# Dilated mixers with masks added by TensorE and the softmax read from PSUM; p's upper parts copied bank by bank

## The chip, the core and the metric

The kernel runs on one core of a Trainium2 chip. The core has five instruction queues that run beside each other and wait for each other by semaphores: TensorE (PE in the profile; PEld is its weight load), VectorE (DVE), ScalarE (ACT), GpSimd (POOL) and SyncE (SP, which issues DMAs). Each queue runs its instructions in order. The metric is device microseconds of one execution.

## The reference, cut to what matters

Two models run one after the other on 1024 positions of width 1024, all in fp32. The first has a differential attention layer (layer 0) and a latent attention layer (layer 1, MLA: 8 heads, softmax over the whole row of 1024 keys). The second has a block with three mixers (A: spatial gating, B: stick-breaking attention, 6 heads, C: dilated attention, 6 heads in 3 groups) and a feed-forward part (FFN). The two softmaxes that the change touches:

```python
# MLA, a head and a block of 128 queries
p = softmax((qn @ kn.T + qp @ kpe.T) * scale); o = p @ v

# mixer C, dilation d = 1, 4, 16 by group: each query sees itself and up to 128 keys, d apart, before it
z = where(valid, (q * k_gathered).sum(-1) * 0.125, -inf)
z_max = z.max(-1); p = exp(z - z_max); denom = p.sum(-1)
o = (p @ v_gathered) / denom;  lse = z_max + log(denom)
alpha = softmax(lse over the 3 groups);  y_c = o * alpha
```

## The kernel before, in words

Every fp32 operand of a product is split into an upper part, rounded to the type that TensorE reads fast (F32R), and a rest, the lower part; a product is two or three matmuls of such parts. The split of a tile in PSUM is an ACT copy (the upper part) and a DVE subtraction (`lo`, the lower part). In the profile a split of p is "ACT CAST pt<-m" and "DVE TENSOR_TENSOR pt<-m,pt".

The order on each engine is not written by hand: the kernel is written as generators that are merged, and a scheduler then sets the order of the instructions by a simulated timeline and priorities. So a change of one function can move instructions anywhere near. PSUM is held by four pools: tiles s (scores, two buffers of two banks), m (four buffers of one bank), t and u (two each). A tile's buffer is free for the next tile when its last reader is done. All instructions go through one wrapper at line 111, so the profile's rows all carry L111 and are told apart by tiles: s scores, e the row of exponentials, pt the split p, v the values, cf small columns of numbers, cr the identity matrix, kk/qq mixer keys and queries, h the split keys and queries of MLA, wr/wh/wl weights as loaded and their upper and lower part, tf/tb/z/t/ab work tiles.

In time order: layer 0 runs to about 1040 us, layer 1 with MLA to 1500 us, its output product and the mixers' start to 1630 us, the dilated mixers C to about 1830 us, mixer B to 2100 us, then the FFN.

MLA (`mla_attention`): for each head and block of 128 queries, 10 matmuls write a tile s of 128x1024 scores; DVE takes the row maximum from PSUM, ACT the exponential from PSUM with its sum; POOL multiplies by the reciprocal of the sum; `pt_fill` then transposes p with TensorE, four blocks of 128 columns into one bank m, twice for a row. For each bank it issues copy, lo, copy, lo: one pair for the first two blocks and one for the others. Mixer B uses the same `pt_fill`; layer 0 doesn't.

Mixer C (`mixer_c_attention`): three groups with dilations d = 1, 4 and 16, two heads e in each, two halves of four query blocks in each head; so 12 halves, of which the 8 with d < 16 are wide (256 key columns a block) and 4 narrow (128). Each half makes its scores with two matmuls a block in a tile s (`score`, start to stop), copies them to SBUF with ACT (one copy for the own blocks, one for the blocks before), masks the copies with GpSimd (`affine_select`, `memset`), and then runs maximum, subtraction, exponential, sum on DVE, DVE, ACT, DVE. After both halves of a head come the logarithm (ACT), a scalar_tensor_tensor and a reciprocal (DVE), all into one small tile `ld` with a single buffer, and DMAs on SyncE's queue that scatter its two halves into a DRAM tensor lse. So a second head's logarithm and reciprocal wait until the first head's DMAs have read `ld`. When the third group is done, `alphas_c` loads lse back and takes the softmax over the groups on DVE and ACT.

The change also touches `mask_tile`, which makes mixer B's triangular mask, and `load`, which gives a tile whose first uses in a part of the program are tied to a column `sign` by a small GpSimd copy, so that they can't be made earlier than that column.

## Time and profile before

| | us |
|---|---|
| runs of the kernel | 2916.08, 2925.15, 2933.8 (median 2925.15) |
| profiled execution, its own time | 2909.92 |
| its span (first to last instruction) | 2907.9 |
| TensorE busy / VectorE / ScalarE / GpSimd in the span | 2629.5 / 2099.3 / 1421.6 / 1292.2 |
| mean granted TensorE clock, share of full speed | 0.956 |

TensorE is busy for 90% of the span, VectorE for 72%, ScalarE for 49%, GpSimd for 44%. Times in the rows are microseconds from the span's start. An idle stretch of an engine is put down to the engine whose work ended it. The granted clock is 1.0 at 2.4 GHz and 0.5 at 1.2 GHz; a stretch's value is the mean.

### The profile page before, as it was taken

What the parts mean: (1) busy time and instruction counts of PE and PEld (TensorE: products, weight loads), DVE (VectorE), ACT (ScalarE), POOL (GpSimd) and SP (SyncE); (2) the same over time, 40 slices, a digit from 0 to 9 for tenths busy, and PEclk for the clock granted to TensorE, in tenths of its full rate; (3) what the DMA queues carried; (4) which work ended last, traced back from release to release, by engine and by line L of the source; (5) the groups of instructions that cost most, each with busy time, mean ns of one, the idle gap of its engine ahead of it and who ended that gap; (6) DMA issues with size and microseconds to landing.
All of it is one profiled execution on the core that took longest, in us unless ns stands there. A gap on an engine that the chain in (4) does not pass through costs nothing. (4 is left out here: it accounts for less than half of the span.)

```text
span 2907.9 us, 34523 instructions
## 1 busy us (share of the span) xinstructions
PE 2629.5 (90%) x12023; PEld 2128.7 (73%) x12023; DVE 2099.3 (72%) x2696; ACT 1421.6 (49%) x2609; POOL 1292.2 (44%) x779
## 2 busy tenths in 40 slices
PE   7899999998899979999997798887978999997897
PEld 4678787887777867877775687776766777776676
DVE  7577877778642596667768563778768888899865
ACT  5455555556444534544554453667544344443432
POOL 2423323342344532212243332444447878778761
PEclk8999999999999999999998999999989999998998
DMA  7233333234541473223342356332621222234564
GB/s 292 66 97 101 109 109 105 66 95 141 174 131 42 127 254 106 71 89 118 117 132 80 80 82 112 91 87 85 197 89 51 88 79 73 87 124 146 187 237 147
DMA packets 308402, 338.91 MB, mean 117 GB/s; under 512 B 37428, under 2 KB 232068, under 8 KB 308228
## 3 DMA queue, kind: packets, MB, share of 16 engines
q1 hardware_dynamic: 308228, 336.69, 39.3%
q8 instruction: 96, 1.57, 0.2%
q14 instruction: 78, 0.64, 0.1%
HBM read 231.17 MB, written 60.89 MB: 100 GB/s over the span
## 5 line engine op out<-in xcount | busy, mean ns | idle before, releaser
L111 PE MATMUL m<-h,wh 128*128 128x512 f32 x3480 | 985.0, 402 | 48.1 <-DVE h L111 14.4
L111 PEld LDWEIGHTS m<-h,wh 128*128 128x128 f32 x3480 | 669.4, 194 | 204.2 <-DVE h L111 18.2
L111 POOL TENSOR_TENSOR wl<-wr,wh 128x1024 fp32r<-128x1024 f32 (+1 forms) x146 | 333.5, 2291 | 429.6 <-ACT wh L111 393.4
L111 PE MATMUL u<-h,wh 128*128 128x512 f32 x1264 | 408.3, 404 | 1.4 <-ACT h L111 0.8
L111 POOL TENSOR_SCALAR e<-e,cf 128x1024 f32<-128x1024 f32 x128 | 152.6, 1193 | 564.8 <-DVE cf L111 403.5
L111 PE MATMUL m<-h,wl 128*128 128x512 f32 x840 | 336.8, 402 | 7.8 <-POOL wl L111 7.8
L111 ACT ACTIVATE e<-s,cf 128x1024 f32<-128x1024 f32 x192 | 216.0, 1126 | 240.4 <-DVE cf L111 221.9
L111 ACT CAST wh<-wr 128x1024 fp32r<-128x1024 f32 (+3 forms) x252 | 202.6, 810 | 170.1 <-PE m L111 67.7
L111 DVE TENSOR_REDUCE cf<-s 128x1 f32<-128x1024 f32 x192 | 228.3, 1217 | 69.6 <-PE s L111 69.2
L111 PEld LDWEIGHTS u<-h,wh 128*128 128x128 f32 x1264 | 233.1, 191 | 47.5 <-ACT h L111 1.2
L111 PE MATMUL u<-h,wl 128*128 128x512 f32 x632 | 252.5, 400 | 12.7 <-POOL wl L111 12.7
L111 PE MATMUL s<-kk,qq 128*128 128x512 f32 (+3 forms) x752 | 187.3, 386 | 35.8 <-DVE e L111 18.7
L111 ACT CAST pt<-m 128x256 fp32r<-128x256 f32 (+2 forms) x396 | 140.1, 376 | 155.1 <-PE m L111 88.4
L111 PE MATMUL s<-h,wh 128*128 128x512 f32 x720 | 182.8, 399 | 35.5 <-DVE h L111 18.2
L111 PEld LDWEIGHTS m<-h,wl 128*128 128x128 f32 x840 | 164.1, 195 | 44.5 <-POOL wl L111 9.0
L111 DVE SCALAR_TENSOR_TENSOR e<-z,cf,e 128x1023 f32<-128x1023 f32 (+1 forms) x88 | 175.8, 2008 | 24.8 <-ACT e L111 24.6
L111 PE MATMUL s<-h,h 128*128 128x512 f32 x640 | 171.5, 414 | 20.8 <-DVE h L111 14.3
L111 PEld LDWEIGHTS s<-h,wh 128*128 128x128 f32 x720 | 136.5, 192 | 71.3 <-DVE h L111 19.7
L111 DVE TENSOR_TENSOR pt<-m,pt 128x256 fp32r<-128x256 f32 (+2 forms) x396 | 155.0, 416 | 41.6 <-ACT pt L111 34.6
L111 PEld LDWEIGHTS s<-kk,qq 128*128 128x128 f32 x752 | 135.9, 196 | 65.8 <-DVE e L111 20.4
L111 PE MATMUL m<-pt,v 128*128 128x512 f32 (+3 forms) x668 | 151.9, 371 | 17.1 <-ACT pt L111 8.6
L111 PEld LDWEIGHTS s<-h,h 128*128 128x128 f32 x640 | 122.3, 196 | 52.5 <-DVE h L111 17.8
(285 smaller groups left out, 4848.0 us busy)
## 6 DMA issues: line engine op xcount, KB each, us to landing
wr<-in_w_in_dram SPq DMA_DIRECT2D x61, 512.0 KB
wr<-in_w_out_dram SPq DMA_DIRECT2D x48, 512.0 KB
tb<-in_w_ada_dram SPq DMA_DIRECT2D x48, 512.0 KB
wr<-in_w_up_dram SPq DMA_DIRECT2D x47, 512.0 KB
qq<-ab SPq DMA_DIRECT2D x144, 128.0 KB
wr<-in_ada_w_dram SPq DMA_DIRECT2D x32, 512.0 KB
tf<-act SPq DMA_DIRECT2D x30, 512.0 KB
wr<-in_w_down_dram SPq DMA_DIRECT2D x30, 512.0 KB
```

What stands on the lines that cost most here:

```text
L111: ins = f(*args, **kw)
```

## The change

Three functions change, and one is new.

`pt_fill`: the upper parts of a bank are copied one behind the other, then the lower parts are taken: copy, copy, lo, lo in place of copy, lo, copy, lo. The number of instructions stays.

`mixer_c_attention`: in each block of a half an additional matmul of the identity with a mask tile comes first (start) and writes 0 or a large negative number, and the two score matmuls add to it. DVE takes the maximum straight from PSUM and a small scaling by -0.125 of it; four exponentials (ACT, one for each block, since the bias is a column for each block) read PSUM, write the tile e and give the sums. The ACT copies, GpSimd's masks and memsets on the scores, the DVE subtraction and the DVE sum go.

`masks_c` (new): five mask blocks made on GpSimd in a tile z at the mixers' start and copied by ACT into a tile tb that stays for all three groups.

`mask_tile`: its tile comes from `load`, so the mask for mixer B is made at the mixers' start and not at the program's.

```diff
@@ -280,7 +280,7 @@
     def mask_tile(self, name, op, pattern, mult):
 
         nc = self.nc
-        m = self.t("t2", [128, 128])
+        m = self.load("t2", [128, 128])
         nc.gpsimd.memset(m, 0.0)
         nc.gpsimd.affine_select(m, m, pattern, op, -BIG, base=0, channel_multiplier=mult)
         out = self.c([128, 128], name, F32R)
@@ -820,11 +820,11 @@
             for i in range(n):
                 kt = 4 * g + i
                 nc.tensor.transpose(ps[:, i], p[:, kt * 128:(kt + 1) * 128], self.ident)
-            for i in range(0, n, 2):
-                m = min(2, n - i)
-                hi, lo = (pts[4 * g + i + x][:, 0:m, qs] for x in range(2))
-                nc.scalar.copy(hi, ps[:, i:i + m])
-                self.lo(lo, ps[:, i:i + m], hi)
+            parts = [(pts[4 * g + i], pts[4 * g + i + 1], i, min(2, n - i)) for i in range(0, n, 2)]
+            for hi, _, i, m in parts:
+                nc.scalar.copy(hi[:, 0:m, qs], ps[:, i:i + m])
+            for hi, lo, i, m in parts:
+                self.lo(lo[:, 0:m, qs], ps[:, i:i + m], hi[:, 0:m, qs])
 
     def pv(self, v, pts):
 
@@ -1826,7 +1826,21 @@
             qf = [lambda hl, j, s=s: qt[s][hl][:, j * 128:j * 128 + 128] for s in range(2)]
         box += [kk, qf]
 
-    def mixer_c_attention(self, g, d, kk, q, vbox, lse, od):
+    def masks_c(self):
+
+        nc = self.nc
+        m = self.load("z", [128, 5, 128])
+        nc.gpsimd.memset(m, 0.0)
+        nc.gpsimd.affine_select(m[:, 0], m[:, 0], [[1, 128]], ALU.is_ge, -BIG, base=0, channel_multiplier=-1)
+        for i in (1, 3, 4):
+            nc.gpsimd.affine_select(m[:, i], m[:, i], [[-1, 128]], ALU.is_ge, -BIG, base=0, channel_multiplier=1)
+        nc.gpsimd.memset(m[:, 2], -BIG)
+        nc.gpsimd.memset(m[64:128, 4, 0:64], -BIG)
+        out = self.t("tb", [128, 5, 128], F32R)
+        nc.scalar.copy(out, m)
+        return out
+
+    def mixer_c_attention(self, g, d, kk, q, vbox, lse, od, masks):
         nc = self.nc
         y = self.t("z", [128, S])
         wide = d < 16
@@ -1838,33 +1852,24 @@
                 np_ = 2 if wide else 1
                 ps = self.pS((128, 4, 256))
                 z = self.t("e", [128, 4, np_, 128])
-                for i, j in enumerate(js):
-                    k0 = j * 128 - (128 if prev(j) else 0)
-                    o = ps[:, i, 256 - (j * 128 + 128 - k0):256]
-                    self.score(o, q[e], j, kk[e], slice(k0, j * 128 + 128))
-                own = z[:, :, np_ - 1]
-                nc.scalar.copy(own, ps[:, :, 128:256])
-                nc.gpsimd.affine_select(own, own, [[0, 4], [-1, 128]], ALU.is_ge, -BIG, base=0, channel_multiplier=1)
-                if not wide:
-                    nc.gpsimd.memset(own[64:128, :, 0:64], -BIG)
-                else:
-                    sel = [i for i, j in enumerate(js) if prev(j)]
-                    off = [i for i in range(4) if i not in sel]
-                    sl = slice(sel[0], sel[-1] + 1, sel[1] - sel[0])
-                    pz = z[:, sl, 0]
-                    nc.scalar.copy(pz, ps[:, sl, 0:128])
-                    nc.gpsimd.affine_select(
-                        pz, pz, [[0, len(sel)], [1, 128]], ALU.is_ge, -BIG, base=0, channel_multiplier=-1)
-                    for i in off:
-                        nc.gpsimd.memset(z[:, i, 0], -BIG)
-                z3 = z.rearrange("p j a k -> p j (a k)")
                 wd = np_ * 128
                 zm = stat[:, half * 4:half * 4 + 4]
                 den = stat[:, 8 + half * 4:12 + half * 4]
-                nc.vector.reduce_max(zm, z3, axis=AX)
-                nc.vector.tensor_sub(z3, z3, zm.rearrange("p (j o) -> p j o", o=1).to_broadcast([128, 4, wd]))
-                nc.scalar.activation(z3, z3, AF.Exp, scale=0.125)
-                nc.vector.reduce_sum(den, z3, axis=AX)
+                nm = self.small(4, "ss")
+                for i, j in enumerate(js):
+                    m = (0 if prev(j) else 2) if wide else 4
+                    nc.tensor.matmul(ps[:, i, 256 - wd:256], self.ident_r, masks[:, m:m + np_], start=True, stop=False)
+                    k0 = j * 128 - (128 if prev(j) else 0)
+                    ks = slice(k0, j * 128 + 128)
+                    o = ps[:, i, 256 - (j * 128 + 128 - k0):256]
+                    nc.tensor.matmul(o, q[e](0, j), kk[e][:, ks], start=False, stop=False)
+                    nc.tensor.matmul(o, q[e](1, j), kk[e][:, ks], start=False, stop=True)
+                zs = ps[:, :, 256 - wd:256]
+                nc.vector.reduce_max(zm, zs, axis=AX)
+                nc.vector.tensor_scalar_mul(nm, zm, -0.125)
+                for i in range(4):
+                    nc.scalar.activation(z[:, i].rearrange("p a k -> p (a k)"), zs[:, i], AF.Exp, bias=nm[:, i:i + 1],
+                                         scale=0.125, accum_out=den[:, i:i + 1])
                 parts = [[i for i, j in enumerate(js) if prev(j)] if a_ == 0 and wide else list(range(4))
                          for a_ in range(np_)]
                 o = self.pm()
@@ -1944,6 +1949,7 @@
 
         vcol = lambda i: 2432 + i * 128 if i < 3 else 1280 + (i - 3) * 128
         self.off_b = self.mask_tile("off_b", ALU.is_gt, [[-1, 128]], 1)
+        masks = self.masks_c()
         ma = self.mixer_a(w, hts, od)
         def qkv(i, box, vbox):
             yield from qk(i, box)
@@ -1957,7 +1963,7 @@
             cur, cv, box, vbox = box, vbox, [], []
             nxt = qkv(i + 1, box, vbox)
             if i < 3:
-                att = self.mixer_c_attention(i, dil[i], *cur, cv, lse, od)
+                att = self.mixer_c_attention(i, dil[i], *cur, cv, lse, od, masks)
                 merge(ahead(self.tc, att, HP_C), alternate(ma, nxt) if i == 0 else nxt, LEAD_C)
             else:
                 att = self.mixer_b_attention(i - 3, *cur, cv, od)
```

The instructions of all engines stand in the same order up to about 1055 us (layer 1's first head) and again from about 2190 us on (the FFN); between them the scheduler has set another order. TensorE has 48 more matmuls (7066 rows of the order for 6999), VectorE 2610 rows for 2625, ScalarE 2342 for 2356, GpSimd 754 for 776.

Three places show it, all on VectorE's queue. The first stands before layer 1's last head, before and then after; pt are the lower parts of p, m_11977 and m_11986 the two banks of one row of p, h the lower part of that head's queries and keys, cf<-s a row maximum:

```order
L111 TENSOR_TENSOR pt_11892<-m_11977,pt_11891 128x2x128
L111 TENSOR_TENSOR pt_11896<-m_11986,pt_11895 128x2x128
L111 TENSOR_TENSOR h_2006_12055<-tf_12053,h_2006_12055 128x512
L111 TENSOR_TENSOR h_2007_12058<-tf_12053,h_2007_12058 128x512
L111 RECIPROCAL cf<-cf 128x1
L111 TENSOR_REDUCE cf<-s_12334 128x1
L111 TENSOR_SCALAR cf<-cf 128x1
L111 TENSOR_TENSOR h_2013_12098<-tf_12096,h_2013_12098 128x512
L111 TENSOR_REDUCE cf<-s_12407 128x1
L111 TENSOR_TENSOR h_2014_12101<-tf_12096,h_2014_12101 128x512
L111 TENSOR_TENSOR pt_11894<-m_11977,pt_11893 128x2x128
L111 TENSOR_TENSOR pt_11898<-m_11986,pt_11897 128x2x128
```

```order
L111 TENSOR_TENSOR pt_11892<-m_11977,pt_11891 128x2x128
L111 TENSOR_TENSOR pt_11894<-m_11977,pt_11893 128x2x128
L111 TENSOR_TENSOR pt_11896<-m_11986,pt_11895 128x2x128
L111 TENSOR_TENSOR pt_11898<-m_11986,pt_11897 128x2x128
L111 TENSOR_TENSOR h_2006_12055<-tf_12053,h_2006_12055 128x512
L111 TENSOR_TENSOR h_2007_12058<-tf_12053,h_2007_12058 128x512
L111 TENSOR_REDUCE cf<-s_12261 128x1
L111 RECIPROCAL cf<-cf 128x1
L111 TENSOR_SCALAR cf<-cf 128x1
L111 TENSOR_TENSOR h_2013_12098<-tf_12096,h_2013_12098 128x512
L111 TENSOR_REDUCE cf<-s_12334 128x1
L111 TENSOR_TENSOR h_2014_12101<-tf_12096,h_2014_12101 128x512
```

The second subtractions of both banks stood ten rows behind the first ones; now the four follow each other, ahead of the work on h.

The second place is the end of the first head's softmax in the second dilated group (d=4). RECIPROCAL and SCALAR_TENSOR_TENSOR on cf of 128x8 write `ld`, tf are the rotated queries and keys of the next group, z the head's output; tile numbers differ between the two kernels by a small offset (z_13969 is z_13989). Before, and then after:

```order
L111 TENSOR_TENSOR z_13969<-m_14271,t_2359_14304 64x512
L111 RECIPROCAL cf<-cf 128x8
L111 SCALAR_TENSOR_TENSOR cf<-cf 128x8
L111 SCALAR_TENSOR_TENSOR tf_14384<-m_14358,tb_12737 128x512
L111 TENSOR_TENSOR tf_14383<-m_14358,tb_12736 128x512
L111 TENSOR_REDUCE cf<-e_14729 128x4
L111 SCALAR_TENSOR_TENSOR cf<-cf 128x8
L111 TENSOR_TENSOR tf_14444<-m_14394,tb_12736 128x512
L111 TENSOR_TENSOR tf_14445<-m_14394,tb_12737 128x512
L111 RECIPROCAL cf<-cf 128x8
```

```order
L111 SCALAR_TENSOR_TENSOR cf<-cf 128x8
L111 TENSOR_REDUCE cf<-s_14726 128x4
L111 TENSOR_SCALAR cf<-cf 128x4
L111 RECIPROCAL cf<-cf 128x8
L111 SCALAR_TENSOR_TENSOR cf<-cf 128x8
L111 TENSOR_TENSOR z_13989<-m_14281,t_2361_14314 64x512
L111 TENSOR_TENSOR tf_14393<-m_14343,tb_12736 128x512
L111 TENSOR_TENSOR tf_14394<-m_14343,tb_12737 128x512
L111 SCALAR_TENSOR_TENSOR tf_14394<-m_14368,tb_12737 128x512
L111 TENSOR_TENSOR tf_14393<-m_14368,tb_12736 128x512
```

Before, the second head's RECIPROCAL (the last row) stood behind four rows on tf; now it stands (fourth row) three rows behind the row that ends the first head's `ld`, and ahead of the z row and all four tf rows.

The third place is the end of the third group (d=16), second head. tb and e of 128x128 to 128x384 belong to mixer B, ab to mixer B's projections. Before, and then after:

```order
L111 TENSOR_REDUCE cf<-e_15098 128x4
L111 TENSOR_REDUCE cf<-e_15137 128x4
L111 SCALAR_TENSOR_TENSOR tb_15206<-cf,tb_15206 128x128
L111 SCALAR_TENSOR_TENSOR tb_15264<-cf,tb_15264 128x256
L111 TENSOR_TENSOR e_15098<-e_15098,cf 128x512
L111 TENSOR_TENSOR e_15137<-e_15137,cf 128x512
L111 SCALAR_TENSOR_TENSOR tb_15281<-cf,tb_15281 128x384
L111 TENSOR_REDUCE cf<-e_15098 128x4
L111 TENSOR_REDUCE cf<-e_15137 128x4
L111 TENSOR_TENSOR z_14926<-m_15037,t_2467_15054 64x8x64
L111 RECIPROCAL cf<-cf 128x8
L111 SCALAR_TENSOR_TENSOR cf<-cf 128x8
```

```order
L111 TENSOR_REDUCE cf<-s_15133 128x4
L111 TENSOR_REDUCE cf<-s_15093 128x4
L111 TENSOR_SCALAR cf<-cf 128x4 x2
L111 RECIPROCAL cf<-cf 128x8
L111 TENSOR_TENSOR z_14493<-m_14746,t_2428_14773 64x2x256
L111 SCALAR_TENSOR_TENSOR cf<-cf 128x8
L111 SCALAR_TENSOR_TENSOR ab_14823<-m_14798,ab_14823 128x512
L111 SCALAR_TENSOR_TENSOR ab_14851<-m_14826,ab_14851 128x512
L111 SCALAR_TENSOR_TENSOR ab_14889<-m_14864,ab_14889 128x512
L111 TENSOR_TENSOR pt_14947<-m_14942,pt_14947 128x512
L111 TENSOR_SCALAR e_15201<-s_15197 128x128
L111 SCALAR_TENSOR_TENSOR ab_14917<-m_14892,ab_14917 128x512
```

Before, the second head's softmax stood between rows of mixer B, and `alphas_c`'s first reduce 12 rows behind the last row shown; now it stands ahead of all of mixer B, and that reduce 27 rows behind its SCALAR_TENSOR_TENSOR on cf (the sixth row).

## Rows read from the trace of the kernel before

**Rows 1.** Busy time of the engines in stretches of the span: from:to, length, then busy us of each engine with its instructions, TensorE's granted clock as a share of full speed, DMA share and GB/s.

```profile
1100.00:1200.00 100.00, 96.02 (x489) 79.50 (x488) 67.05 (x140) 48.81 (x117) 21.64 (x21) 0.98 0.32 94
...
1630.00:1830.00 200.00, 185.56 (x936) 156.04 (x937) 106.00 (x139) 85.28 (x138) 62.20 (x55) 0.95 0.56 104
1830.00:2120.00 290.00, 246.45 (x1200) 203.65 (x1199) 231.98 (x317) 189.07 (x369) 128.05 (x70) 0.94 0.40 115
```

**Rows 2.** Waits from 1100 to 1500 us (layer 1's attention), all engines: engine and the tile it wrote, the engine waited for and the tile that it wrote, us in total, times, longest.

```profile
ACT pt L111 <- DVE pt L111: 44.2, 49, 2.4
...
DVE pt L111 <- ACT pt L111: 24.0, 30, 3.0
...
PE s L111 <- DVE h L111: 8.5, 3, 3.5
...
PE m L111 <- DVE v L111: 3.4, 1, 3.4
```

**Rows 3.** The same view as rows 1, for three short stretches just behind long waits of TensorE (two in layer 1's attention, one at the start of mixer B).

```profile
1140.40:1143.80 3.40, 3.40 (x12) 2.82 (x11) 3.40 (x6) 0.97 (x3) 0.00 (x0) 0.50 0.80 272
...
1433.90:1440.70 6.80, 5.90 (x18) 4.67 (x19) 5.98 (x17) 3.35 (x9) 2.23 (x2) 0.50 1.00 339
1853.80:1860.60 6.80, 5.39 (x14) 4.43 (x15) 6.55 (x13) 4.82 (x12) 1.44 (x2) 0.50 0.31 86
```

**Rows 4.** Timeline of VectorE from 1424 to 1434 us, before layer 1's last head: start, us, engine, operation, out<-in, shape, count [idle before <- releaser].

```profile
1424.83 0.75 DVE L111 TENSOR_TENSOR pt<-m,pt 128x256 fp32r<-128x256 f32 x2
...
1428.17 2.86 DVE L111 TENSOR_TENSOR h<-tf,h 128x512 fp32r<-128x512 f32 x1
...
1432.68 0.74 DVE L111 TENSOR_TENSOR pt<-m,pt 128x256 fp32r<-128x256 f32 x2
...
1434.08 0.67 DVE L111 TENSOR_TENSOR v<-m,v 128x512 fp32r<-128x512 f32 x1
```

**Rows 5.** The same view of TensorE at 1434.8 us.

```profile
1434.80 1.12 PE L111 MATMUL m<-cr,e 128*128 128x128 f32 x4 [3.37 <-DVE v L111]
```

**Rows 6.** Instructions grouped by form from 1630 to 1835 us (the dilated mixers): line, engine, operation, out<-in, shape, count | busy us, mean ns | idle before.

```profile
L111 DVE TENSOR_REDUCE cf<-e 128x4 f32<-128x1024 f32 x16 | 19.3, 1216 | 5.8 <-POOL e L111 3.1 <-ACT e L111 2.6
...
L111 DVE TENSOR_TENSOR e<-e,cf 128x1024 f32<-128x1024 f32 x8 | 9.7, 1220 | 0.0
L111 POOL TENSOR_SCALAR_AFFINE_SELECT e<-e 128x512 f32<-128x512 f32 x14 | 9.1, 666 | 18.6 <-ACT e L111 18.6
...
L111 ACT ACTIVATE e<-e 128x1024 f32<-128x1024 f32 x8 | 8.4, 1060 | 8.2 <-DVE e L111 8.2
...
L111 ACT COPY e<-s 128x512 f32<-128x512 f32 x14 | 7.9, 604 | 5.7 <-PE s L111 3.9 <-remote 1.8
...
L111 DVE TENSOR_REDUCE cf<-e 128x4 f32<-128x512 f32 x8 | 5.1, 675 | 0.2 <-ACT e L111 0.2
...
L111 DVE TENSOR_TENSOR e<-e,cf 128x512 f32<-128x512 f32 x4 | 2.8, 748 | 0.0
...
L111 ACT ACTIVATE e<-e 128x256 f32<-128x256 f32 x1 | 0.4, 418 | 0.1
```

**Rows 7.** The same view from 1060 to 1500 us (layer 1's attention): operations that read PSUM (tile s), the read of the accumulator, and a small scaling.

```profile
L111 DVE TENSOR_REDUCE cf<-s 128x1 f32<-128x1024 f32 x59 | 72.0, 1220 | 31.5 <-PE s L111 31.1
...
L111 ACT ACTIVATE e<-s,cf 128x1024 f32<-128x1024 f32 x60 | 67.3, 1124 | 59.6 <-DVE cf L111 51.3 <-DMA tf<-od 6.5 <-issue 1.8
...
L111 ACT ACTIVATION_READ_ACCUMULATOR e<-s,cf 128x1 f32 x60 | 12.1, 201 | 0.0
...
L111 DVE TENSOR_SCALAR cf<-cf 128x1 f32<-128x1 f32 x60 | 8.3, 146 | 0.5
```

**Rows 8.** Timeline of TensorE, the 16 score matmuls of one half of the first dilated group.

```profile
1654.45 2.04 PE L111 MATMUL s<-kk,qq 128*128 128x256 f32 x16
```

**Rows 9.** Timeline of all engines in the second dilated group (d=4), 1744 to 1771 us; cf are the small columns, lse the row-wise log-sums in DRAM, SPq SyncE's queue of DMA issues.

```profile
1744.79 0.21 ACT L111 ACTIVATE cf<-cf 128x8 f32<-128x8 f32 x1
...
1747.99 19.75 SPq L111 DMA_DIRECT2D lse<-cf  x8
...
1756.81 0.21 ACT L111 ACTIVATE cf<-cf 128x8 f32<-128x8 f32 x1 [9.97 <-DMA lse<-cf]
...
1761.45 0.37 PE L111 MATMUL m<-pt,v 128*128 128x128 f32 x1 [4.21 <-ACT pt L111]
...
1765.92 0.20 DVE L111 RECIPROCAL cf<-cf 128x8 f32<-128x8 f32 x1 [7.50 <-DMA lse<-cf]
...
1770.39 0.78 PE L111 MATMUL m<-pt,v 128*128 128x128 f32 x5 [2.37 <-DVE pt L111]
```

**Rows 10.** The same view where mixer B begins, 1834 to 1858 us.

```profile
1836.20 3.02 SPq L111 DMA_DIRECT2D lse<-cf  x4
...
1836.29 0.30 PE L111 MATMUL m<-cr,tf 128*128 128x128 f32 x1 [1.67 <-ACT cf L111]
...
1852.15 0.21 DVE L111 TENSOR_REDUCE cf<-t 128x16 f32<-128x48 f32 x1 [6.65 <-DMA t<-lse]
...
1855.21 1.54 PE L111 MATMUL s<-kk,qq 128*128 128x512 f32 x4 [6.43 <-DVE e L111]
```

**Rows 11.** Waits as in rows 2, from 1850 to 2120 us (mixer B).

```profile
PE s L111 <- DVE e L111: 18.6, 12, 6.4
...
ACT pt L111 <- DVE pt L111: 7.1, 6, 2.1
...
DVE pt L111 <- ACT pt L111: 5.8, 10, 1.4
```

## The prediction

> **What bounds the kernel now.** I read busy time by stretches first. In layer 1's attention TensorE is busy 96.0 of 100 us, in the dilated mixers 185.6 of 200, in mixer B 246.5 of 290, while VectorE there is at 232.0 of 290 [rows 1]. So TensorE bounds all three, and mixer B is nearly bound by VectorE as well. What can be won is TensorE's idle time and time at the half clock; work taken from VectorE, ScalarE or GpSimd is worth only the waits of TensorE that it ends.
>
> Second, waits. In layer 1, ScalarE waits 44.2 us for VectorE's part of the split of p, 49 times, and VectorE 24.0 us for ScalarE's, 30 times: they alternate on one bank. But TensorE itself waits for other things: 8.5 us in 3 waits on h and 3.4 us in one wait put down to v [rows 2]. These sit where one head passes to the next, and the granted clock is 0.50 behind them, for 3.4 us at 1140 and 6.8 us at 1434 [rows 3]. The last of them can be followed: the first lower parts of two banks are taken at 1424.83, then come h, maxima and more h, one of them 2.86 us long, and the second lower parts of the same banks only at 1432.68 [rows 4]. Until then both m buffers are held, and TensorE stands for 3.37 us until 1434.80 [rows 5]; v, which ends beside it, is only the name that the view gives.
>
> Third, the timelines of the dilated mixers. In the group d=4 the first head's logarithm runs at 1744.79, its DMAs begin to issue at 1747.99, the second head's logarithm waits 9.97 us for them until 1756.81 and the reciprocal 7.50 us until 1765.92. TensorE stands 4.21 us until 1761.45 and 2.37 until 1770.39 [rows 9]. Where mixer B begins, the last scatter issues at 1836.20, VectorE stands 6.65 us until the loaded lse lets the reduce of `alphas_c` run at 1852.15, and TensorE 6.43 us until 1855.21 [rows 10], with 6.8 us at clock 0.50 [rows 3].
>
> **Split of p, layer 1.** Nothing is added; the four subtractions of two banks stand together, and the banks come free where the first pair did. The 3.37 us wait and about as much as one of the others (8.5 us in 3) may go in part: behind them the new order on TensorE still meets h, which I leave where it is. A stretch of 3.4 us at clock 0.50 does the work of 1.7 us, so each avoided one is worth 1.7 us. There are four such passes of heads. I take 1.4 us of waiting less in two of them, none in the third and 3.4 in the last, 6.2 together, and one half-clock stretch of 3.4 us less (1.7): **-8 us**. Bounds: at least the last wait alone gets shorter by half (-2); at most all of the 8.5 + 3.4 us and 6.8/2 + 3.4/2 us of clock go (-17). ScalarE's 44.2 us of waits go nearly whole, but ScalarE has half its time free there (48.8 of 100) [rows 1], and TensorE doesn't wait for them: worth nothing by themselves.
>
> **Dilated mixers, TensorE.** 12 halves with four blocks give 48 mask matmuls. 16 score matmuls of 256 columns took 2.04 us [rows 8], 0.13 each; 48 x 0.13 = 6.1 us at most (a third of them have 128 columns), I take **+5.5**, all on the path.
>
> **Dilated mixers, VectorE.** Gone are 8 subtractions of 1.22 and 4 of 0.75, 8 sums of 1.22 and 4 of 0.68 us [rows 6]: 9.8 + 3.0 + 9.7 + 2.7 = 25.2. Added are 12 small scalings of 0.15 [rows 7], 1.8. The maximum reads PSUM in 1.220 against 1.216 us from SBUF [rows 6, 7], so it costs the same. Net -23.4 us on an engine that is busy 106 of 200 us there: worth only the waits below. On this the Trainium skill, Perfetto Trace Analysis, section Optimizing Scalar/DVE Operations, states more overhead for VectorE on PSUM (about 125 ns) than on SBUF (about 60 ns); by that the 12 maxima would cost 0.8 us more. The two rows show no such difference, and I go by them; neither would move the sum.
>
> **ScalarE and GpSimd.** A wide half gives up a copy of 0.60, a second one of at most that, and an exponential of 1.06 us; it gets four of 0.42 from SBUF [rows 6] with four reads of the accumulator of 0.20, half or all of them beside the next exponential [rows 7]: 1.7 to 2.5 us for 1.7 to 2.3. About nothing, on an engine busy 85 of 200 us [rows 1]. GpSimd loses 14 masks of 0.67 us and more [rows 6], some 15 us with the memsets, and gets five small masks at the mixers' start, at most 5 x 0.67 = 3.4 us; it is 62 us busy of 200 and TensorE waits for none of it: nothing.
>
> **The chain of a half.** Before: copy 0.60, mask 0.67, maximum 1.22, subtraction 1.22, exponential 1.06 = 4.8 us ahead of the transposes, and 1.22 for the sum before the logarithm. Now: maximum 1.22, scaling 0.15, four exponentials 1.7 to 2.5 = 3.1 to 3.9. On the other side a tile s was free after 0.6 to 1.2 us of copies and is now held through the last exponential, about 3 us, with two buffers. The third half of a pair of heads then waits for the first one's exponentials. I bound that from 0 to 2 us for each of four such places and put it into the groups below.
>
> **Group by group.** d=1: the waits in it are small; I take -1.5, from the shorter chain. d=4: the first logarithm no longer stands behind four sums and subtractions interleaved with the second head's; about 6 such steps of 1.22, so it comes 7 to 8 us earlier, at 1737. But the RECIPROCAL of the second head now stands ahead of the z row and four tf rows. By the rows it is free 17.9 us after the first issue (1747.99 to 1765.92), so about 1758 to 1759. TensorE reaches the place at 1757.2 (1761.45 - 4.21), and 3 us later by its mask matmuls. So VectorE is freed about when TensorE comes; then tf and ScalarE's copies must follow. I take the same stalls as before, **0**, from -4 (the 4.21 us go) to +8 (below). d=16: the second head's softmax stands ahead of mixer B, its lse is stored earlier against B's rows, and the reduce has 27 rows ahead of it in place of 12. The 6.43 us wait goes, half of the 6.8 us at half clock with it (-3.4), and the 1.67 us wait at 1836.29 [rows 10]: -11.5. Together +5.5 - 1.5 + 0 - 11.5 = -7.5; I add -1.5 for smaller waits, **-9 us** (from +8 - 3 = +5, the d=4 stall grown and the d=16 wait only halved, to -20).
>
> **Mixer B.** The same `pt_fill`, but only 7.1 us of ScalarE's waits are on it, and TensorE waits 18.6 us for VectorE's e, of which 6.4 are counted above [rows 11]. VectorE is the scarce one, and its work isn't less. **-3 us** (+5 to -8: the two lower parts now come in a row of 0.8 us ahead of the scores' reading).
>
> **Sum.** -8 - 9 - 3 = -20 us: the profiled execution's 2909.9 becomes 2890. That execution lies 15 us under the median of the runs, 2925.15, so on the runs' scale I forecast **2905 us**.
>
> **Rivals.** (a) The waits move and don't go. TensorE is at 93 to 96% where most of the change lies; with layer 1 at -2, d=16 at -6 and the masks paid in full at +5.5 the sum is about -3: 2922. For it: the waits at the passes of heads end on h, which the change doesn't hasten. Against it: the 6.43 us wait has a cause that the new order plainly moves.
>
> (b) Slower: `ld` in the group d=4. If the first logarithm comes no earlier than before, VectorE stands at the second RECIPROCAL until 1765.9 with z and four tf rows (0.7 us each) and behind them ScalarE's copies of pt; TensorE's wait at 1757.2 + 3 becomes 1765.9 + 2.8 + 4 - 1760.2 = 12.5 us for the 6.6 of before, +6; the same block at d=16 holds four projections' sums in m, +4; the s buffers +6; the masks +5.5. With layer 1 at -2 and d=16's gain at -6 the sum is +14: 2939. It decides at whether the logarithm comes at least 6 us earlier. The order of the rows speaks against it: between the last maximum and the logarithm nothing of VectorE's is left.
>
> (c) More than I took: the passes of heads lose all their waits and half-clock stretches (-17), d=16 as above, mixer B gets VectorE's time earlier (-8): about -35, 2890. The rule behind this one is that two engines must not be at one bank together: ScalarE's and VectorE's 44.2 and 24.0 us of mutual waits show it. The Trainium skill, PSUM — Partial Sum Buffer, states it as a collision of engines on a bank, reads included; the trace agrees in that the two alternate.
>
> (d) The change doesn't do what it says: the waits of ScalarE on VectorE's pt stay, since another order of the scheduler brings them back. Then layer 1 gives 0 and the rest -12: 2913.
>
> **How the numbers follow.** A change of under 0.5% (14.6 us) can't be told from none here. Forecast, -15 to -27: 0.42. (c): 0.14. (a) and (d), within 14.6 us either way: 0.30. (b): 0.14. Faster by over 0.5%: 0.42 + 0.14 = 0.56, less 0.01 for its edge: 0.55; the same 0.31; slower 0.14. The range: the bounds add to -17 - 20 - 8 = -45 and -2 + 5 + 5 = +8, which don't all come together; with two in ten left out, -43 to +7: 2882 to 2932.
>
> **What would show it.** In the changed profile: waits of ScalarE on VectorE's pt in layer 1 under 10 us in place of 44.2; no wait of over 3 us of TensorE near 1434; 48 mask matmuls at 0.11 to 0.13 us; the first logarithm of d=4 18 us or more ahead of TensorE's arrival, or a long wait of VectorE at the second RECIPROCAL if (b) holds; no wait of TensorE of 6 us at mixer B's start. I would be wrong if the mask matmuls cost more than 0.2 us each, or if the longer hold of s shows waits of TensorE on ScalarE's e in the dilated mixers of over 6 us together.

## The result, and the profile after

| | before | changed |
|---|---|---|
| runs, median (lowest to highest), us | 2920.61 (2910.64 to 2933.8) | 2888.82 (2886.01 to 2896.87) |
| profiled execution, its own time | 2909.92 | 2886.01 |
| its span | 2907.9 | 2884.3 |
| TensorE busy / VectorE / ScalarE / GpSimd | 2629.5 / 2099.3 / 1421.6 / 1292.2 | 2620.6 / 2061.8 / 1415.1 / 1288.2 |

The ratio of the runs is 0.9895 (95% interval 0.9861 to 0.9929): faster by 1.05%, some 31 us. The two profiled executions differ by 24 us. The forecast was 2905 us, or 20 us less, in a range from 2882 to 2932.

Where the 24 us lie is read from windows whose ends are the same matmuls in every trace: layer 1's first scores, its last product with v, the first scores of the dilated mixers, the first of mixer B, and the first rows of the FFN that are the same again. Columns as in [rows 1]. The kernel before, in the execution that the prediction was made from:

```profile
1028.80:1479.70 450.90, 421.05 (x2074) 345.14 (x2075) 320.03 (x610) 220.23 (x498) 115.28 (x95) 0.96 0.39 120
1479.70:1630.10 150.40, 113.92 (x454) 90.29 (x452) 107.50 (x114) 71.62 (x112) 57.53 (x34) 0.89 0.32 97
1630.10:1826.30 196.20, 181.86 (x917) 152.78 (x917) 102.59 (x132) 82.26 (x131) 60.67 (x52) 0.95 0.56 103
1826.30:2208.40 382.10, 316.28 (x1468) 257.04 (x1467) 290.71 (x382) 224.69 (x433) 179.04 (x105) 0.93 0.35 102
```

The changed kernel:

```profile
1026.20:1450.30 424.10, 410.01 (x2073) 336.02 (x2074) 307.69 (x611) 214.19 (x498) 120.22 (x95) 0.99 0.42 128
1450.30:1602.60 152.30, 115.15 (x457) 91.93 (x455) 107.31 (x113) 72.87 (x114) 60.25 (x44) 0.89 0.32 96
1602.60:1800.50 197.90, 180.68 (x923) 152.51 (x923) 86.39 (x126) 84.40 (x197) 47.17 (x22) 0.95 0.57 95
1800.50:2184.40 383.90, 321.06 (x1508) 263.39 (x1506) 290.24 (x376) 223.05 (x430) 177.37 (x102) 0.92 0.37 105
```

Layer 1 takes 424.1 us for 450.9, and the mean clock there is 0.99 for 0.96. The other stages take 1 to 2 us more. So layer 1 gave 26.8 us, not 8, and the dilated mixers seem to have given nothing. The second half of this reading turned out to be in part an accident of one execution, as the trace of "before again" shows below.

It is in part one of the windows too, since the last two don't hold the same work. The third has 46 matmuls with the mask in the changed kernel, but only 6 matmuls more (923 for 917): 40 others, 24 of them m<-h,wh and m<-h,wl, now stand behind mixer B's first score and are counted in the fourth (1508 for 1468). So these two windows are better read together: 581.8 us for 578.3.

Layer 1's waits in the changed kernel, from 1075 to 1475 us; they answer to [rows 2]:

```profile
ACT pt L111 <- PE m L111: 77.6, 39, 5.6
...
DVE pt L111 <- ACT pt L111: 23.4, 21, 2.7
...
PE m L111 <- DVE pt L111: 4.5, 5, 1.8
```

ScalarE's 49 waits for VectorE's pt, 44.2 us, are gone altogether, and so are TensorE's on h; the longest wait that TensorE has left up to layer 1's end at 1450.3 is 1.8 us. VectorE's waits for ScalarE's pt stay (23.4 us for 24.0). Of the half-clock stretches behind the passes of heads [rows 3] none is left: from 1040 us to the layer's end the granted clock is 1.00.

The dilated group d=4, answering to [rows 9]; SPq is SyncE's queue:

```profile
1715.01 0.21 ACT L111 ACTIVATE cf<-cf 128x8 f32<-128x8 f32 x1 [7.70 <-DMA lse<-cf]
...
1715.45 18.17 SPq L111 DMA_DIRECT2D lse<-cf  x6
...
1726.68 0.20 DVE L111 RECIPROCAL cf<-cf 128x8 f32<-128x8 f32 x1 [9.92 <-DMA lse<-cf]
1731.98 0.21 ACT L111 ACTIVATE cf<-cf 128x8 f32<-128x8 f32 x1 [13.11 <-DMA lse<-cf]
...
1734.90 1.22 PE L111 MATMUL m<-h,wh 128*128 128x512 f32 x2 [8.24 <-DVE tf L111]
```

The stall that the prediction feared is there: VectorE stands 9.92 us at the second head's RECIPROCAL until the first head's scatter has read the small buffer, ScalarE 13.11 us at its logarithm, TensorE 8.24 us. The first head's logarithm too, at 1715.01, had waited 7.70 us, for the scatter of the group d=1. Mixer B's waits, answering to [rows 11]:

```profile
PE m L111 <- DVE pt L111: 8.9, 5, 7.7
PE m L111 <- ACT tf L111: 8.8, 3, 5.7
...
PE m L111 <- DVE t L111: 6.3, 2, 5.6
...
PE s L111 <- DVE e L111: 5.7, 6, 2.2
```

The 6.43 us wait at mixer B's start [rows 10] is gone and s<-DVE e fell from 18.6 to 5.7 us, but single waits of 7.7, 5.7 and 5.6 us stand later in the mixer, and its window, with 40 matmuls more, is as long as before.

### The profile page after: what moved, and what is told of

It reads as the page before. It is cut to its first block, busy times and chain, and to the rows that moved or that the text cites. A ratio compares the mean times of both kernels' runs of the same rounds, so it can differ in the third digit from the quotient of the medians.

```text
span 2884.3 us, 34732 instructions
## 1 busy us (share of the span) xinstructions
PE 2620.6 (91%) x12071; PEld 2126.2 (74%) x12071; DVE 2061.8 (71%) x2684; ACT 1415.1 (49%) x2674; POOL 1288.2 (45%) x754
## 5 line engine op out<-in xcount | busy, mean ns | idle before, releaser
L111 ACT ACTIVATE e<-s,cf 128x1024 f32<-128x1024 f32 (+2 forms) x240 | 236.4, 989 | 258.6 <-DVE cf L111 233.3
L111 DVE TENSOR_REDUCE cf<-s 128x1 f32<-128x1024 f32 (+2 forms) x204 | 240.4, 1206 | 88.1 <-PE s L111 87.6
L111 PEld LDWEIGHTS u<-h,wh 128*128 128x128 f32 x1264 | 232.9, 191 | 47.2 <-ACT h L111 1.2
L111 PEld LDWEIGHTS m<-h,wl 128*128 128x128 f32 x840 | 162.7, 194 | 44.2 <-POOL wl L111 9.2
L111 ACT CAST pt<-m 128x256 fp32r<-128x256 f32 (+2 forms) x396 | 126.1, 387 | 110.3 <-PE m L111 108.5
L111 DVE TENSOR_TENSOR pt<-m,pt 128x256 fp32r<-128x256 f32 (+2 forms) x396 | 146.3, 416 | 42.0 <-ACT pt L111 38.8
L111 PE MATMUL s<-h,h 128*128 128x512 f32 x640 | 165.4, 404 | 9.5 <-DVE h L111 5.8
L111 POOL TENSOR_TENSOR tf<-tf,tf 128x1024 f32<-128x1024 f32 (+1 forms) x50 | 105.1, 2107 | 134.7 <-DVE tf L111 109.9
```

Source lines behind the costliest of these rows:

```text
L111: ins = f(*args, **kw)
```

## The experiments

Medians and ratios are against the kernel before on the same chip; its own median was between 2920.6 and 2921.9 us for e1 to e10, and 2930.5 us for e11.

### e1 and e2: each half of the change alone

e1 is the kernel before with the new `pt_fill`; e2 is the changed kernel with the old one. e2 against the changed kernel:

```diff
-            for hi, _, i, m in parts:
-                nc.scalar.copy(hi[:, 0:m, qs], ps[:, i:i + m])
-            for hi, lo, i, m in parts:
-                self.lo(lo[:, 0:m, qs], ps[:, i:i + m], hi[:, 0:m, qs])
+            for i in range(0, n, 2):
+                m = min(2, n - i)
+                hi, lo = (pts[4 * g + i + x][:, 0:m, qs] for x in range(2))
+                nc.scalar.copy(hi, ps[:, i:i + m])
+                self.lo(lo, ps[:, i:i + m], hi)
```

> The kernel before with the new order of copies and subtractions alone (copy, copy, lo, lo in a bank); mixer C as before. Theory A: nearly the whole gain comes from layer 1, since the changed trace reaches the last scores of layer 1 at 1406.8 us in place of 1428.6, with 3.4 us at half clock from 1060 to 1500 us in place of five stretches of 27.2 us; the rest of the program gives nothing in sum. Then this is faster than before by 20 to 30 us (ratio 0.990 to 0.993), and its dilated mixers have the waits of before. Theory B, as predicted: layer 1 gives 8 us, mixer B 3, and the dilated mixers the rest; then 8 to 12 us faster (ratio about 0.996).

> The changed kernel with the old order of copies and subtractions (copy, lo, copy, lo); the dilated mixers new. Theory A: 48 mask matmuls cost 5 to 6 us, and what the mixers save in waits pays just that, so the time is that of before within 5 us (ratio 0.998 to 1.002). Theory B, as predicted: 9 us faster (ratio 0.997), with no wait of 6 us at the start of mixer B.

Measured: e1 2893.61 us, ratio 0.991 (0.9887 to 0.9933); e2 2910.89 us, ratio 0.9965 (0.9953 to 0.9978). The split alone gives some 26 us, as theory A had it. But e2 is 10 us faster, as theory B had it, and outside theory A's range. Each theory was right about one of the two, so "the mixers give nothing" falls. The windows of layer 1 and of the dilated mixers, first e1, then e2:

```profile
1032.00:1459.80 427.80, 411.40 (x2073) 337.29 (x2074) 308.23 (x611) 214.68 (x498) 120.51 (x95) 0.98 0.42 127
1612.20:1816.50 204.30, 182.71 (x917) 154.27 (x917) 104.88 (x132) 82.62 (x131) 60.66 (x52) 0.93 0.54 99
```

```profile
1029.30:1477.80 448.50, 419.69 (x2074) 343.42 (x2075) 317.90 (x611) 219.66 (x498) 115.92 (x95) 0.97 0.39 121
1630.70:1829.30 198.60, 183.04 (x923) 154.51 (x923) 86.05 (x126) 84.14 (x197) 46.44 (x22) 0.93 0.58 94
```

Layer 1 is short only where the split is new (427.8 against 448.5). The dilated mixers take 198.6 us in the new form, but 204.3 in e1, where they are those of before, not the 196.2 of the first trace.

### before again: how far executions of one kernel differ

> The kernel before once more, for a second trace: the first one's execution, 2909.9 us, lies 11 us under the median of all runs. It shows by stage how far executions of one program differ, so which differences between traces mean something: expected within 3 us in each stage, with the differences in half-clock stretches and not in the work.

Measured: 2922.99 us, near the median. By stage (the stretch between layer 1 and the mixers is left out):

```profile
1029.30:1479.60 450.30, 420.66 (x2074) 344.61 (x2075) 320.24 (x610) 220.07 (x498) 115.25 (x95) 0.96 0.39 120
...
1630.00:1840.20 210.20, 185.32 (x917) 156.33 (x917) 102.83 (x132) 82.91 (x131) 61.09 (x52) 0.91 0.55 95
1840.20:2221.50 381.30, 318.51 (x1466) 258.50 (x1465) 287.80 (x382) 224.75 (x432) 178.00 (x105) 0.91 0.35 102
```

Layer 1 and mixer B agree with the first trace within 1 us. The dilated mixers do not: 210.2 us for 196.2, with a clock of 0.91 for 0.95. The expectation of 3 us in each stage was wrong there by far. The place is again d=4:

```profile
1748.01 21.13 SPq L111 DMA_DIRECT2D lse<-cf  x8
...
1763.60 0.21 ACT L111 ACTIVATE cf<-cf 128x8 f32<-128x8 f32 x1 [16.85 <-DMA lse<-cf]
...
1768.24 0.47 PE L111 MATMUL m<-pt,v 128*128 128x128 f32 x1 [11.10 <-ACT pt L111]
```

```profile
PE m L111 <- ACT pt L111: 12.4, 4, 11.1
PE s L111 <- DMA qq<-pt: 8.7, 2, 7.7
```

The same four scatters of the first head start at the same time (1748.01, and 1747.99 in [rows 9]), but the logarithm comes free at 1763.60 in place of 1756.81, and TensorE waits 11.10 us for 4.21, and then 8.7 us for the keys and queries of the next group. So the execution that the prediction was made from had the shortest wait of the four traces with the old mixers and one small buffer. The others give 210.2, 204.3 (e1) and 204.0 (e9, below), the changed kernel 197.9. Together with mixer B's window, because of the moved matmuls, it is 591.5, 588.0 and 588.4 us against 581.8, so the new mixers gain 6 to 10 us. This is a rough measure, since the traced executions of e1 and e9 were the slowest of their runs, 9 to 10 us above the medians, and that of the changed kernel the fastest of its four. The runs of e2 are the better one, and they give 10 us (6 to 14).

### e3: three small buffers for the log-sums

```diff
-        ... "ld": (16, 1), ...
+        ... "ld": (16, 3), ...
```

(and 32 more columns in the tile of small columns, COLS 488 to 520)

> The changed kernel with three buffers for the small tile that holds a head's log-sums until its DMAs have read it, in place of one; every engine's order of instructions is the same as in the changed kernel. In the changed kernel's trace VectorE stands 9.92 us at the second head's RECIPROCAL until 1726.68 (for the DMAs) and 5.34 us more behind it, ScalarE 13.11 us until 1731.98, and TensorE 8.24 us until 1734.90, with 6.8 us at half clock. Theory A: that single buffer is where the mixers' gain went; with three it is 8 to 12 us faster than the changed kernel (ratio to before 0.985 to 0.987). Rival: the wait moves to the next late thing (tf on GpSimd, the m buffers), and 0 to 3 us are left (ratio 0.989).

Measured: 2880.65 us, ratio 0.9868 (0.9842 to 0.9893). The waits on the scatter go, as theory A has it:

```profile
1713.50 0.23 ACT L111 ACTIVATE cf<-cf 128x8 f32<-128x8 f32 x1
...
1721.60 0.21 ACT L111 ACTIVATE cf<-cf 128x8 f32<-128x8 f32 x1
1721.60 0.20 DVE L111 RECIPROCAL cf<-cf 128x8 f32<-128x8 f32 x1 [2.06 <-ACT e L111]
```

Both logarithms and the second RECIPROCAL now follow within 8.1 us, with 2.06 us of waiting. But a wait of 5.08 us appears later in the group, put down to ScalarE's pt:

```profile
1755.74 0.48 PE L111 MATMUL m<-pt,v 128*128 128x128 f32 x1 [5.08 <-ACT pt L111]
```

By the medians 8 us are gained on the changed kernel. The intervals of the two ratios overlap, so it is likely and not certain.

### e4: the split taken row by row

```diff
+        parts = []
         for g in range((ktiles + 3) // 4):
...
-            parts = [(pts[4 * g + i], pts[4 * g + i + 1], i, min(2, n - i)) for i in range(0, n, 2)]
+            parts += [(pts[4 * g + i], pts[4 * g + i + 1], ps[:, i:i + min(2, n - i)], min(2, n - i)) for i in range(0, n, 2)]
-            for hi, _, i, m in parts:
+        for hi, _, src, m in parts:
...
```

> The changed kernel with the split taken over a whole row of p: the copies of both banks first, then the four subtractions. Each bank is held longer by the other's copies (0.3 to 0.7 us), and ScalarE and VectorE alternate once a row in place of twice. If the gain of the new order is that banks come free earlier (theory A1), this gives some of it back: 3 to 10 us slower than the changed kernel. If it is that the two engines no longer alternate (theory A2), it is the same or up to 5 us faster.

Measured: 2883.72 us, ratio 0.9867 (0.9844 to 0.989). Not slower, so the 3 to 10 us of theory A1 aren't there: holding the first bank longer by the other's copies costs nothing that is shown. This says little of the kernel before, where the second lower parts came ten rows later. A2's number fits, and the 5 us by the medians lie within the intervals; but that the end of the alternation is the cause isn't shown by it, and e9 below speaks against it.

### e5: each mask matmul twice

```diff
                     nc.tensor.matmul(ps[:, i, 256 - wd:256], self.ident_r, masks[:, m:m + np_], start=True, stop=False)
+                    nc.tensor.matmul(ps[:, i, 256 - wd:256], self.ident_r, masks[:, m:m + np_], start=False, stop=False)
```

> The changed kernel with each mask matmul of the dilated mixers issued twice, so 48 matmuls more; the second adds the same mask again. The prediction's price: 5.5 to 6.1 us more than the changed kernel, all on TensorE's path (ratio to before about 0.9915). Rival: the mixers' pace is set by the log-sums' DMAs and not by TensorE, and the 48 matmuls fill waits: 0 to 2 us more (ratio 0.9895).

Measured: 2887.59 us, ratio 0.9891 (0.9869 to 0.9912): the same as the changed kernel. The rival's number came out, but its reason is only half right:

```profile
1611.10:1805.90 194.80, 185.06 (x1000) 158.80 (x1001) 90.13 (x126) 84.49 (x190) 48.22 (x22) 0.98 0.61 95
```

TensorE is busy 185.1 us in the dilated mixers for 180.7 in the changed kernel. These 4.4 us aren't the price of the masks: the window has 77 matmuls more (1000 for 923), 46 with the mask and 31 that the changed kernel does in mixer B, and its clock is 0.98 for 0.95. The 8.24 us wait of d=4 isn't in this trace; the scheduler's order is another around it. So the price on the path is not separated by this run.

### e6: mixer B with the old split

The old function stands beside the new one, and mixer B calls it:

```diff
-                    self.pt_fill(pts, u, slot, qi + 1)
+                    self.pt_fill_pair(pts, u, slot, qi + 1)
```

> The changed kernel in which mixer B alone keeps the old order copy, lo, copy, lo; layer 1 has the new one, and all engines have the same order up to mixer B. By the prediction mixer B gained 3 us: this is 3 us slower than the changed kernel (ratio 0.9905). By the traces (382.1 us from mixer B's first score to the FFN before, 383.9 after) it gained nothing: the same within 2 us, or a little faster.

Measured: 2887.55 us, ratio 0.9885 (0.9863 to 0.9906): the same. No gain of mixer B from the split is shown; the 3 us lie just inside the interval's upper end.

### e7: row-wise and three buffers

The edits of e3 and e4 together on the changed kernel, no others.

> The row-wise split of e4 and the three small buffers of e3 together on the changed kernel. If the two are independent: 5 + 8 us less than the changed kernel, about 2875 us (ratio 0.983 to 0.985). If both only shorten the same waits in the dilated mixers: as e3 or e4 alone (0.987).

Measured: 2879.81 us, ratio 0.9863 (0.9839 to 0.9887). By the medians as e3 or e4 alone; the interval reaches into the 0.983 to 0.985 of a full sum, so that the two don't add is likely and not certain.

### e8: the old order, with a bank for each pair

```diff
+        for k in range(0, ktiles, 2):
+            m = min(2, ktiles - k)
+            ps = self.pm((128, 2, 128))
+            for i in range(m):
+                nc.tensor.transpose(ps[:, i], p[:, (k + i) * 128:(k + i + 1) * 128], self.ident)
+            hi, lo = (pts[k + x][:, 0:m, qs] for x in range(2))
+            nc.scalar.copy(hi, ps[:, 0:m])
+            self.lo(lo, ps[:, 0:m], hi)
```

> The changed kernel with the old order copy, lo, copy, lo, but each pair of blocks transposed into a bank of its own (four m tiles for a row in place of two). Theory A2a: ScalarE waited for VectorE because both read one bank, not because of the order as such; then ScalarE's waits on VectorE's pt (46.9 us in 55 before) are gone in layer 1 with the old order too, and its gain stays as far as four m buffers allow: from the changed kernel's time to 10 us more (ratio 0.989 to 0.993). Rival A2b: the waits come from the order of the two queues; then they are there again and layer 1 takes its 450 us (ratio 0.996 to 1.0).

Measured: 2934.28 us, ratio 1.0044 (1.0027 to 1.0061). ScalarE's waits on pt:

```profile
ACT pt L111 <- PE m L111: 130.0, 62, 5.8
DVE pt L111 <- ACT pt L111: 41.1, 19, 5.0
```

ScalarE doesn't wait for VectorE's pt once, with copy, lo, copy, lo as before. So those waits came from the two engines' reading one bank (or one tile, which the edit changed with it), and not from the order as such: A2a's mechanism is shown. VectorE's waits for ScalarE's pt are no part of it, since its subtraction reads ScalarE's copy: they stay, 41.1 us. ScalarE's own waiting isn't less either: it waits 130.0 us for the transposes, for 66.8 + 53.1 us on transposes and VectorE's pt before in the same window. And A2a's time is not shown: 45 us more than the changed kernel. Layer 1:

```profile
1025.00:1487.00 462.00, 428.09 (x2073) 343.00 (x2074) 308.56 (x610) 217.69 (x498) 115.91 (x95) 0.96 0.38 117
```

Here TensorE is busy 428.1 us for 410.0 at a clock of 0.96. TensorE itself waits 13.2 us for VectorE's pt here, for 1.3 us before. That four tiles for a row are too many for four m buffers would explain these waits, but no run tried it, and why the same matmuls are busy longer was not followed. So e8 shows what made ScalarE's waits, and not what ending them is worth.

### e9 and e10: five tiles tb in layer 1

What stands ahead of the passes was then read again in the trace before, around 1139 us; z<-tb,cf,z is a step of the second model's modulation on VectorE, whose weights are loaded into tb:

```profile
1133.62 1.28 DVE L111 SCALAR_TENSOR_TENSOR z<-tb,cf,z 128x1024 f32<-128x1024 f32 x1 [1.53 <-DMA tb<-in_w_ada_dram]
...
1138.54 0.69 DVE L111 TENSOR_TENSOR h<-m,h 128x512 fp32r<-128x512 f32 x1
...
1139.28 1.19 PE L111 MATMUL s<-h,h 128*128 128x512 f32 x4 [2.53 <-DVE h L111]
```

The step waits 1.53 us for a DMA of the weights, and the subtraction for h, which TensorE waits for until 1139.28, stands behind it in the queue. The tiles tb are three, so a load waits until an earlier step has read its tile.

```diff
-    ... ab=3, pt=12, e=6, v=3, z=3, wr=4, wh=3, wl=3, tb=3, t2=2, tf=4),
+    ... ab=3, pt=12, e=6, v=3, z=3, wr=4, wh=3, wl=3, tb=5, t2=2, tf=4),
```

> The kernel before, with five buffers in place of three for the tiles tb of layer 1, into which the adaptive weights are loaded for VectorE's modulation. In the trace before, VectorE's modulation waits 1.53, 1.88 and 2.94 us for those loads just ahead of three passes of heads, and the subtraction for h, which TensorE waits for, stands behind it in VectorE's queue. Theory T2: that wait is what made TensorE late at the passes, and the new split only covered it; then this gains 8 to 15 us with the old split (ratio 0.995 to 0.997) and three of the four passes lose their half clock. Theory T1: the passes are late because the banks of p are held and the order of TensorE puts scores ahead of projections; then the waits on h stay and the time is that of before within 3 us.

> The changed kernel with three small buffers for the log-sums (e3) and five tiles tb in layer 1 (e9). If the loads still cost something with the new split (its trace has waits of 0.39 to 0.95 us there), 1 to 4 us less than e3, about 2878 us; if not, as e3 (ratio 0.9868).

Measured: e9 2900.32 us, ratio 0.9938 (0.9918 to 0.9958), with the old split; e10 2879.62 us, ratio 0.9872 (0.9844 to 0.99), as e3. Waits of e9 in layer 1, then its windows of layer 1 and of the dilated mixers:

```profile
ACT pt L111 <- DVE pt L111: 47.2, 57, 2.4
...
PE m L111 <- DVE v L111: 3.3, 1, 3.3
...
PE s L111 <- DVE h L111: 1.2, 3, 0.4
```

```profile
1034.80:1466.30 431.50, 412.27 (x2074) 338.88 (x2075) 313.12 (x607) 219.46 (x496) 112.87 (x93) 0.98 0.39 121
1618.40:1822.40 204.00, 183.03 (x916) 154.62 (x917) 102.87 (x132) 82.75 (x131) 61.08 (x52) 0.93 0.54 98
```

Layer 1 takes 431.5 us for 450.9 although ScalarE still waits 47.2 us for VectorE's pt, for 53.1 before in the same window. VectorE's modulation no longer waits for the loads, TensorE's waits on h fell from 8.5 to 1.2 us, and three of the four passes have no half clock behind them. Only the last pass is as before: TensorE still waits 3.3 us on v there. So theory T2's mechanism fits, with a gain of 21 us by the medians for its 8 to 15, and 47 us of ScalarE's waiting for VectorE cost TensorE little.

Two reservations. With five tiles the scheduler sets another order in layer 1 too, so e9 shows that the tiles for the loads decide, not how much of it is the shorter wait and how much the order. And the wait for a load alone doesn't make a pass late: in e1 VectorE waits 1.60 us for one just ahead of the pass at 1230 us, but TensorE has four projections (m<-qq,wh) and two more (m<-qq,wl) ahead of the scores at 1236.47 and doesn't wait on h.

### e11: the two buffer counts without the change

e9's edit and e3's on the kernel before.

> The kernel before with two buffer counts changed and nothing else: five tiles tb in layer 1 (as e9) and three small buffers for the log-sums (as e3). If the waits on these two were what the change mostly took away, this gets most of its gain without it: 21 us from layer 1 (e9) and 8 to 14 us from the dilated mixers, whose waits of TensorE of 10.6 and 11.1 us in the group d=4 (traces of e1 and of before again) go; about 2890 us, ratio 0.986 to 0.990. If the dilated mixers' gain came from the shorter softmax itself, it stays near e9's 0.9938.

Measured: 2901.98 us, ratio 0.9906 (0.9891 to 0.9922), which can't be told from the change's own 0.9895; the time itself, on another chip, is 13 us above the changed kernel's. But the part of the dilated mixers isn't as expected: their wait moved.

```profile
1747.96 0.33 PE L111 MATMUL m<-pt,v 128*128 128x128 f32 x1 [1.49 <-ACT pt L111]
...
1770.14 0.66 PE L111 MATMUL s<-kk,qq 128*128 128x128 f32 x2 [12.45 <-DMA qq<-pt]
```

In d=4 the 11 us wait is 1.49 now, but TensorE stands 12.45 us at the next group's queries, which come by DMA. In absolute terms e11 and e9 are alike (2902.0 and 2900.3 us), and their ratios differ with the kernel before of each session. With the old mixers the small buffer alone gains nothing that is shown.

## Why the prediction was right, and where its terms were not

The time lay in the range and the sign was right; the 20 us forecast were 31 by the runs. That it lay there is in part luck: layer 1 alone went past its own bound of -17, mixer B's 3 us aren't shown, and d=4 gave its 0 although the step behind it failed. The terms, one by one:

**Split of p, layer 1: -8, measured -23 (e1) to -27 (the changed kernel).** The mechanism was right in that the passes of heads are the place, and wrong in the cause. I took three of the waits to end on h, "which I leave where it is". The trace says more: h stands behind a modulation step that waits for a DMA (e9). The new split ended these waits without touching the loads, since the scheduler set another order: around 1129 us in the changed kernel h's subtraction stands one step earlier, and TensorE does a projection (m<-qq,wh) ahead of the scores that need h.

```profile
1124.39 1.28 DVE L111 SCALAR_TENSOR_TENSOR z<-tb,cf,z 128x1024 f32<-128x1024 f32 x1 [0.39 <-DMA tb<-in_w_ada_dram]
...
1128.71 0.68 DVE L111 TENSOR_TENSOR h<-m,h 128x512 fp32r<-128x512 f32 x1
...
1128.94 0.70 PE L111 MATMUL m<-qq,wh 128*128 128x512 f32 x2 [0.76 <-DVE pt L111]
...
1130.39 1.07 PE L111 MATMUL s<-h,h 128*128 128x512 f32 x4
```

VectorE's step waits 0.39 us for its load there, and TensorE reaches the scores at 1130.39, when h is done at 1129.39 (1128.71 + 0.68), without waiting.

The fourth wait (3.37 us, the last head) I followed to the held banks of p, and called v only a name. That was misread. The second lower parts of p end at 1433.42 (1432.68 + 0.74), but TensorE starts only at 1434.80, 0.05 us behind the end of v's subtraction (1434.08 + 0.67), which reads a tile m as well [rows 4, 5]. So it was v's buffer that was missing, and the pair of p ahead of it in VectorE's queue held it up by its 0.74 us at most. In the changed kernel TensorE does ten score matmuls (from 1404.66, 2.58 us) ahead of these transposes, and 0.36 us of the wait are left:

```profile
1407.60 0.66 PE L111 MATMUL m<-cr,e 128*128 128x128 f32 x4 [0.36 <-DVE v L111]
```

The bound of -17 was too small on the side of the clock. It counted half clock behind two of the four passes, 6.8/2 + 3.4/2 us; behind the other two there were 6.8 us each in the kernel before:

```profile
1239.40:1246.20 6.80, 5.57 (x15) 4.50 (x16) 5.98 (x11) 1.55 (x5) 0.00 (x0) 0.50 0.82 288
1341.80:1348.60 6.80, 6.03 (x16) 4.86 (x17) 6.38 (x11) 1.02 (x3) 0.00 (x0) 0.50 0.40 147
```

All four are gone. TensorE's busy time in layer 1 fell by 11.0 us for the same matmuls (421.05 to 410.01), and its idle time by 15.8 (29.85 to 14.09), so some 11 of the 26.8 us are clock. I had given the clock 1.7 us, and 5.1 in the bound.

**ScalarE's 44.2 us, worth nothing by themselves: right as far as the runs go.** They went to zero in the changed kernel and in e8, and stayed in e9; the time followed the passes in the changed kernel and in e9. No run took these waits alone away, since e8 changed the number of tiles too.

**Dilated mixers, -9: -10 by the runs of e2; by the traces, with mixer B, +3.5 against the first and -6 to -10 against the other three with the old mixers.** The size held on the runs' scale; how it divides among its parts isn't shown. The trace that I read was the execution with the shortest wait in d=4, so the stall of 9 us that I counted on both sides was mostly 11 + 8.7 on the side before.

**d=4: the same stall, 0.** The stall was as predicted, 8.24 us for the 4.21 + 2.37 and smaller ones of the first trace, at the RECIPROCAL that rival (b) named, where VectorE's long wait was (b)'s sign. The step that failed is the logarithm 7 to 8 us earlier: it ran at 1715.01, 112 us after the first dilated scores, for 115 us before (1744.79 - 1630.1), so 2 to 3 us earlier, since it had to wait for the small buffer itself, held by the scatter of d=1 (7.70 us). The prediction has no term for this wait; without it the logarithm would have come 10 us earlier, an estimate from these rows. Rival (b) put its turning point at 6 us and would have been slower by this. It wasn't, since its other parts didn't come (the d=16 wait is gone, and TensorE's waits on ScalarE's e for the s buffers are 2.5 us in the dilated mixers), and the old form mostly waits longer than in the trace that I read. So the 0 came out by luck.

**Masks +5.5:** where the blocks follow each other in the changed kernel, the next matmul starts 0.11 to 0.12 us after the mask's (1675.92 to 1676.04, 1676.29 to 1676.40), so 48 of them are 5.3 to 5.8 us of TensorE by estimate, as forecast; as a cost of the path not shown apart (e5).

**d=16, -11.5 with its clock:** the wait is gone as the order said. Its worth can't be read from mixer B's window, 383.9 for 382.1 us, which has 40 matmuls more and new waits of 5.6 to 7.7 us, one of them behind a slow subtraction on VectorE (below). These waits came with the split and not with d=16: e1, with the old mixers, has them too (5.7, 5.5 and 6.3 us) beside 5.4 us at mixer B's start, and e6, with the old split in mixer B, has none over 3.8 us there.

**Mixer B, -3: no gain shown** (e6). What its split saves and what the new waits cost can't be told apart.

Of the rivals, (c) came nearest in its time (2890) and in its place: the passes of heads lost their waits and half-clock stretches. The rule that I put behind it isn't shown to be the reason. Of the mutual waits, ScalarE's 44.2 us come from the shared bank (or tile) and are ended by separate ones (e8); VectorE's 24.0 us are not ended. The Trainium skill, PSUM — Partial Sum Buffer, section PSUM bank collisions raise a hardware error, states that accesses of two engines to one bank collide, reads included; e8 agrees with it as far as ScalarE's waits go. But e9 got most of layer 1's gain with ScalarE's waits in place. What stays open: why the changed order meets the loads so much better, since the loads' tiles are three in both; whether it would under another scheduler; and e8's slower TensorE.

## What to carry to other kernels

A wait that is long and frequent can be worth little, and a short one can stand at the head of a queue: before pricing an edit, take each wait of the bounding engine back through the queue of the engine that it names, to the first thing there that waits for a DMA or a buffer. One buffer count (e9, five tiles tb) got some 20 of the rewrite's 31 us here, by ending waits that the rewrite's order had covered. And one profiled execution isn't the kernel: where a stage hangs on small scattered DMAs, take a second trace before its terms are set, since the same program differed by 14 us in one stage of 200.

## What the runs showed of the hardware that was not expected

The time until the scatters of the log-sums free their small buffer differs from one execution to the next: they began to issue within 0.02 us of each other in two executions of one kernel, and the logarithm's wait for them ended 8.8 us later in one (1747.99 to 1756.81) and 15.6 in the other (1748.01 to 1763.60).

A subtraction of 128x512 on VectorE takes 0.68 us, but 2.86 at 1428.17 in the kernel before [rows 4]. GpSimd runs a tensor operation on SBUF beside it:

```profile
1428.10 2.38 POOL L111 TENSOR_TENSOR wl<-wr,wh 128x1024 fp32r<-128x1024 f32 x1
```

The subtraction ends at 1431.03, 0.55 us behind GpSimd's operation (1430.48).

The same in the changed kernel at 2032 us, two subtractions in 5.52 us beside GpSimd's operations (one of them 4.34 us long); right behind them stand the subtractions of p that mixer B's 7.7 us wait ends on:

```profile
2030.27 4.34 POOL L111 TENSOR_TENSOR wl<-wr,wh 128x1024 fp32r<-128x1024 f32 x1
...
2032.37 5.52 DVE L111 TENSOR_TENSOR h<-tf,h 128x512 fp32r<-128x512 f32 x2
```

Contention of the two engines is what these rows suggest; no run here tried it apart.
